# Sliding-window attention in a fused decoder block: transposed scores, no row maximum, a multiplicative decay and a row sum by matmul

## Chip, cores and metric

One Trainium2 chip, eight cores. Each core computes a quarter of one of the two sequences (2048 of 8192 positions), with no exchange between cores: the 128 positions before its own come in as an extra input. The metric is the device time of the slowest core in microseconds. Executions of a kernel agree to about 0.3% except that now and then one die, once both, runs at a lower granted clock and takes longer. Such slow runs are left out of all ratios. The medians quoted are over all runs of a kernel; the slow ones among them raise a median by at most 0.4 us, except for a_all, where only the fast runs are quoted.

## The reference, cut to what matters

```
u = rms_norm(h, norm_mix)
z = u @ w_in                       # pool input, q, k, v, two gates
y_pool = pool_mixer(u_pool, ...) @ p_pool
y_attn = swa_sink_attention(q, k, v, sinks) @ p_attn
h = h + (sigmoid(z_gp) * y_pool + sigmoid(z_ga) * y_attn) @ w_out
h = h + relu(rms_norm(h) @ w_up)**2 @ w_down
return rms_norm(h)

# swa_sink_attention: 8 query heads of 64, 2 key heads, blocks of 128 queries
# on 256 keys (previous block and own), window of 128
s = q k / 8 - slope[head] * dist         # -1e30 outside the window
m = max(max over keys of s, sink)
p = exp(s - m) / (sum exp(s - m) + exp(sink - m))
o = p @ v
```

Two identities allow the change. Subtracting m cancels between numerator and denominator, so it may be left out as long as the exps stay in range. And exp(s - slope * dist) = exp(s) * exp(-slope * dist), where the second factor depends only on head and position in the block, so it can be computed once.

## The kernel before

A core goes through stages: norm, transposes and the projections with the pooling mixer (to about 134 us in the trace), attention over 16 blocks (to 240.5), the gated mix, the output projection with the second norm, and the MLP. Only the attention stage and what it feeds on change. A helper records every operation and puts a semaphore wait wherever two engines touch the same buffer; each engine then executes its own stream in the order of the program, as the traces show (VectorE's timeline before repeats sink maximum, multiply, four additions, reduction, reciprocal, copy every 5.85 us, the order in which the loop below issues them). The parts concerned:

```python
BIAS[:, h, :]  = DM * -SLOPES[h]               # VectorE, 16 of these at the start

def att_s1(b):                                 # queries on partitions
    for h in range(8):
        mm(bank(h % 4)[...256 columns], QT[head h, block b], K or KS[256 keys])
    for j in range(4):
        tt("dve", asb[:, j:8:4, :], bank(j), bt[:, j:8:4, :], ALU.add)   # fp32
    reduce_max(mx, asb)                                                  # VectorE
def att_tiny(b):    # max with the sink, its negative, sink - max  (VectorE, POOL)
def att_exp(b):
    for h in range(8):
        act(apb[:, h, :], asb[:, h, :], AF.Exp, bias=ng[:, h], accum=rsum[:, h])
    act(es, es, AF.Exp)
def att_tr(b):      # 16 transposes of 128x128 probabilities into PSUM
def att_ptevac(b):  # 2 ScalarE copies of 128x1024 back to SBUF
def att_pv(b):      # 16 matmuls: probabilities as weights, V as 64 columns
    den = rsum + es; rd = reciprocal(den)
def att_s4_on(b):   # one VectorE multiply 128x512 from PSUM
def att_s4_t(b):    # 4 transposes of the output
def att_s4_evac(b): # VectorE copy of these into QT

for i in range(20): # blocks i .. i-3 in flight
    att_tiny(i-1); att_ptevac(i-2); att_exp(i-1); att_s4_on(i-3); att_s1(i)
    att_s4_t(i-3); att_pv(i-2); att_tr(i-1); att_s4_evac(i-3)
```

## Time and profile before

| | before |
|---|---|
| median of 15 runs | 940.48 us (the five runs at the time of the prediction: 939.69) |
| span of the profiled run, slowest core (core 2) | 937.0 us |
| attention stage on that core | 133.9 to 240.5 us |
| period of one block | 5.85 us |
| in a block: ScalarE busy, VectorE busy | 5.85 us, 5.75 us |
| granted clock in the stage | 0.55 |

How to read it: the page's slices show what is busy when, but not what ends last. A table of stretches gives each engine's busy time in one period of a stage: as long as an engine is busy for the whole period, the period cannot get shorter without less work on that engine. The groups say which instructions fill it, and the timeline's brackets (idle time before an instruction, and who ended it) say where one engine waits for another. In the views PE is TensorE's matmuls, PEld its weight loads, DVE VectorE, ACT ScalarE, POOL GpSimdE; L399 is a line of the kernel, often that of a helper that many operations share. The granted clock is the share of full speed at which TensorE ran. The prediction shows the lines for the kernel before.

### The profile page before, as it was taken

The numbers are of one execution on the slowest core, as the hardware profiler recorded it, in microseconds if no ns is written. First come the engines' busy times: TensorE is split into PE (matmuls) and PEld (weight loads), VectorE is DVE, ScalarE is ACT, GpSimd is POOL, SyncE is SP. The second block draws the span as 40 slices with busy tenths as digits, with TensorE's granted clock in tenths as the row PEclk, the third lists the DMA queues.
The fourth block names the chain that finished last, engine by engine and source line by source line (L and its number), as shares of the span: only waits on it lengthen the run. The fifth ranks groups of instructions, "written<-read, shape, count | busy, mean of one in ns | idle before, by whom it ended". The sixth has DMA issues, their size and how long they took to land.

```text
span 937.0 us, 13763 instructions; the slowest of 8 cores (934.2 to 937.0 us)
## 1 busy us (share of the span) xinstructions
PE 844.7 (90%) x4386; PEld 401.7 (43%) x4441; DVE 392.6 (42%) x582; ACT 320.9 (34%) x678; POOL 208.1 (22%) x236
## 2 busy tenths in 40 slices
PE   1589957887999999999999999999999999999994
PEld 1344423454444444444444444444444444444441
DVE  2372189999222222236542223322223232224545
ACT  2264538999322222235542211112221112223321
POOL 3021731000123232221122111211112111113333
PEclk9999985555799999999999999999999999999997
DMA  9850019300005050069608300560008300001213
GB/s 175 159 181 25 1 21 146 60 2 1 1 1 68 1 68 1 1 147 243 151 23 118 62 1 1 80 100 1 1 1 127 54 1 1 1 1 68 90 69 134
DMA packets 37397, 55.91 MB, mean 60 GB/s; under 512 B 6992, under 2 KB 21584, under 8 KB 37328
## 3 DMA queue, kind: packets, MB, share of 16 engines
q0 software_dynamic: 28816, 27.95, 21.7%
q1 hardware_dynamic: 8512, 27.09, 8.7%
q8 instruction: 37, 0.61, 0.3%
q14 instruction: 32, 0.26, 0.1%
HBM read 74.04 MB, written 8.39 MB: 88 GB/s over the span
## 4 chain that ended last, share of the span: by engine, by line
PE 73%; DVE 9%; issue 7%; ACT 6%; DMA 3%; POOL 1%; DVEq 0%; POOLq 0%; ACTq 0%
PE psum L388 70%; DVE arena L403 6%; ACT arena L399 5%; DMA arena<-w_in 3%; PE psum L392 2%; DVE arena L662 1%; ACT arena L418 1%; DVE arena L408 1%; POOL arena L403 1%; DVE arena L413 0%; POOL arena L423 0%; DVEq L194 0%; ACTq L194 0%; POOLq L280 0%; DVE arena L716 0%
## 5 line engine op out<-in xcount | busy, mean ns | idle before, releaser
L388 PE MATMUL psum<-arena 128*128 128x512 bf16 (+2 forms) x3785 | 781.8, 370 | 33.0 <-DVE arena L403 14.2
L388 PEld LDWEIGHTS psum<-arena 128*128 128x128 bf16 (+1 forms) x3840 | 361.1, 101 | 435.8 <-issue 42.7
L403 POOL TENSOR_TENSOR arena<-arena 128x512 bf16<-128x512 f32 (+3 forms) x199 | 179.8, 910 | 684.0 <-ACT arena L399 291.1
L399 ACT ACTIVATE arena<-psum 128x512 f32<-128x512 f32 (+1 forms) x208 | 123.9, 597 | 450.7 <-PE psum L388 447.7
L403 DVE TENSOR_TENSOR arena<-psum,arena 128x512 f32<-128x512 f32 (+2 forms) x241 | 177.2, 760 | 156.9 <-PE psum L388 122.1
L399 ACT ACTIVATE arena<-arena 128x256 bf16<-128x256 f32 (+2 forms) x209 | 136.8, 673 | 108.4 <-DVE arena L403 51.0
L403 DVE TENSOR_TENSOR arena<-arena 128x512 bf16<-128x512 f32 (+5 forms) x93 | 57.9, 623 | 157.0 <-ACT arena L399 152.6
L392 PE MATMUL psum<-arena 128*128 128x128 bf16 x601 | 75.6, 263 | 46.1 <-DVE arena L408 16.8
L413 DVE SCALAR_TENSOR_TENSOR arena<-arena,psum 128x512 f32<-128x512 f32 x64 | 43.9, 688 | 123.8 <-PE psum L388 120.7
L392 PEld LDWEIGHTS psum<-arena 128*128 128x128 bf16 x601 | 43.8, 111 | 85.7 <-issue 85.2
L418 ACT COPY arena<-psum 128x1024 bf16<-128x1024 bf16 (+4 forms) x57 | 43.4, 808 | 20.6 <-PE psum L388 20.6
L413 DVE SCALAR_TENSOR_TENSOR arena<-arena 128x1024 f32<-128x1024 f32 (+1 forms) x20 | 29.7, 1486 | 39.1 <-POOL arena L403 23.9
L408 DVE TENSOR_SCALAR arena<-arena 128x1 f32<-128x1 f32 (+1 forms) x82 | 24.0, 318 | 35.2 <-ACT arena L399 34.0
L662 DVE TENSOR_REDUCE arena<-arena 128x8 f32<-128x2048 f32 x16 | 36.6, 2286 | 1.7
L399 ACT ACTIVATION_READ_ACCUMULATOR arena<-arena 128x1 f32 x177 | 36.7, 208 | 0.0
L413 DVE SCALAR_TENSOR_TENSOR arena<-psum,arena 128x512 f32<-128x512 f32 x32 | 22.1, 691 | 22.6 <-PE psum L388 22.5
L423 POOL DMA_DIRECT2D arena<-w_in x14 | 12.7, 920 | 16.1 <-DVE arena L403 15.9
L399 ACT ACTIVATE arena<-psum,arena 128x512 bf16<-128x512 f32 x16 | 11.2, 781 | 5.7 <-PE psum L388 4.6
L418 ACT CAST arena<-psum 128x512 bf16<-128x512 f32 (+1 forms) x10 | 5.2, 522 | 18.3 <-PE psum L388 18.3
L423 POOL DMA_DIRECT2D arena<-w_down x4 | 3.5, 884 | 22.7 <-PE psum L388 22.7
L420 DVE COPY arena<-psum 128x512 bf16<-128x512 bf16 x16 | 6.1, 381 | 1.4 <-PE psum L392 1.4
L716 DVE RECIPROCAL arena<-arena 128x8 f32<-128x8 f32 x16 | 3.1, 194 | 2.4 <-POOL arena L403 2.4
(13 smaller groups left out, 14.4 us busy)
## 6 DMA issues: line engine op xcount, KB each, us to landing
arena<-x SPq DMA_DIRECT2D x32, 512.0 KB, 7.9
arena<-w_up POOLq DMA_DIRECT2D x4, 2048.0 KB, 18.7
arena<-w_down POOLq DMA_DIRECT2D x4, 2048.0 KB, 23.7
y<-arena SPq DMA_DIRECT2D x16, 512.0 KB, 2.6
arena<-w_in POOLq DMA_DIRECT2D x9, 512.0 KB, 11.0
arena<-w_out POOLq DMA_DIRECT2D x1, 2048.0 KB, 32.0
arena<-w_in POOLq DMA_DIRECT2D x4, 256.0 KB, 15.4
arena<-w_in POOLq DMA_DIRECT2D x1, 1024.0 KB, 30.1
```

The source lines that it names most:

```text
L388: P.op("pe", lambda e: e.matmul(out, lhsT, rhs, start=start, stop=stop), r=[lhsT, rhs], w=[out])
L392: P.op("pe", lambda e: e.transpose(out, in_, IDENT), r=[in_, IDENT], w=[out])
L399: return e.activation(out, in_, func, bias=bias, scale=scale, **kw)
L403: P.op(eng, lambda e: e.tensor_tensor(out, in0, in1, op), r=[in0, in1], w=[out])
L408: return e.tensor_scalar(out, in0, s1, None, op0)
L413: P.op(eng, lambda e: e.scalar_tensor_tensor(out, in0, scalar, in1, op0, op1), r=[in0, in1] + ([scalar] if isap(scalar) else []), w=[out])
L418: P.op("act", lambda e: e.copy(out, in_), r=[in_], w=[out])
L420: P.op(eng, lambda e: e.tensor_copy(out, in_), r=[in_], w=[out])
L423: P.op(q, lambda e: e.dma_start(out=out, in_=in_), r=[in_], w=[out], dma_slot=slot)
L662: P.op("dve", lambda e: e.reduce_max(mx, asb, AX.X), r=[asb], w=[mx])
L716: P.op("dve", lambda e: e.reciprocal(rd, den), r=[den], w=[rd])
```

## The change

The intent is to take the probability transposes out, and with them the copies, the maximum and the bias additions. Scores are computed transposed (keys on partitions, queries and heads in the free dimension), so the exps already have the orientation that the value matmul wants as weights. A query's maximum over the keys would then lie across partitions, so it is dropped; the bias becomes a factor; the row sum comes from a 65th column of ones in V.

```diff
-    BIAS/BIASZ = -slope * distance         (fp32, VectorE)
+    for h in range(8):                     (bf16, ScalarE)
+        act(EDEC[:, :, h, :], DMv, AF.Exp, scale=-SLOPES[h])
+        act(EDEC0[:, h, :], DMZ, AF.Exp, scale=-SLOPES[h])
+    act(ESINK, SINK, AF.Exp)
...
+    def att_s(b):
+        for kc in range(2):
+            for g in range(2):
+                mm(bank(kc * 2 + g), KT[rows of g, 128 keys], QT[rows of g, 4 heads x 128 queries])
+    def att_exp(b):
+        for kc in range(2):
+            act(ASB[b % 2][...], psum[two banks], AF.Exp, scale=0.125)
+    def att_decay(b):
+        for kc in range(2):
+            for g in range(2):
+                tt("dve", apt[...], asb[...], e[...], ALU.mult)         # 128x512 bf16
+    def att_pv(b):                         # V now has 65 columns, the last is 1
+    def att_norm(b):
+        for g in range(2): den = obank(g)[:, :, 64:65] + ESINK
+        rd = reciprocal(den)
+        for g in range(2): on = obank(g)[:, :, 0:64] * rd
+    def att_ot(b):                         # 4 transposes, one ScalarE copy
+
+    for i in range(19):
+        att_s(i); att_exp(i); att_decay(i-1); att_norm(i-2); att_pv(i-1); att_ot(i-2)
```

On the host side only layouts change: the query columns of w_in are reordered so that a query head sits on the partitions of its key head (which makes the swapped copy of K and its two transfers needless), and the distance tables are transposed.

More of the change, by code (lines that the diff above doesn't have):

```diff
@@ L24 @@
 BUCKET = 1024
-BIAS_TT = True
-TS_MAX = False
-FUSED_MAX = False
 def _esize(dt):
@@ L256, in _build @@
     dm_d = din("dm", [128, 256])
-    dm0_d = din("dm0", [128, 256])
+    dm0_d = din("dm0", [128, 128])
     invc_d = din("invc", [128, 64])
@@ L307, in _build @@
     KT0 = MIX0 + 32768
-    KS0 = KT0 + 4352
-    V0 = KS0 + 4352
-    WOUT0 = V0 + 4352
+    V0 = KT0 + 4352
+    WOUT0 = V0 + 8704
     C0 = WOUT0 + 16384
@@ L318, in _build @@
     KT = sb(KT0, 2176, BF16)
-    KS = sb(KS0, 2176, BF16)
-    V = sb(V0, 17 * 128, BF16).rearrange("p (t k) -> p t k", t=17)
+    V = sb(V0, 17 * 130, BF16).rearrange("p (t g k) -> p t g k", t=17, g=2)
     WOUT = sb(WOUT0, 8 * 1024, BF16).rearrange("p (c n) -> p c n", c=8)
@@ L325, in _build @@
     DM = sb(c, 256, F32); c += 1024
-    DMZ = sb(c, 256, F32); c += 1024
+    DMZ = sb(c, 128, F32); c += 512
+    ESINK = sb(c, 8, F32); c += 32
     G1 = sb(c, 8, F32); c += 32
@@ L344, in _build @@
     WS = [sb(H0 + 49152 + i * 8192, 8 * 512, BF16).rearrange("p (c n) -> p c n", c=8) for i in range(2)]
-    ASB = [sb(H0 + i * 16384, 2048, F32).rearrange("p (h k) -> p h k", h=8) for i in range(2)]
-    APN = [sb(H0 + i * 16384 + 8192, 2048, BF16).rearrange("p (h k) -> p h k", h=8) for i in range(2)]
-    APT = [sb(H0 + i * 16384 + 12288, 2048, BF16).rearrange("p (h k) -> p h k", h=8) for i in range(2)]
+    ASB = [sb(H0 + i * 12288, 2048, BF16).rearrange("p (c n) -> p c n", c=4) for i in range(2)]
+    APT = [sb(H0 + i * 12288 + 8192, 2048, BF16).rearrange("p (c h q) -> p c h q", c=4, h=4) for i in range(2)]
     TG = [[sb(H0 + s * 8192 + j * 2048, 512, F32) for j in range(4)] for s in range(2)]
@@ L371, in _build @@
     st_fix = STAT[:, 16:48]
-    def _stset(j):
-        return [STAT[:, 64 + 64 * i + 8 * j:72 + 64 * i + 8 * j] for i in range(4)]
-    st_mx, st_m8, st_ng, st_rsum, st_es, st_den, st_rd = (_stset(j) for j in range(7))
+    st_den = [STAT[:, 64 + 16 * i:72 + 16 * i] for i in range(2)]
+    st_rd = [STAT[:, 72 + 16 * i:80 + 16 * i] for i in range(2)]
     ON = [sb(H0 + 57344 + i * 1024, 512, BF16) for i in range(2)]
-    MT = sb(H0 + 59392, 1024, F32).rearrange("p (h k) -> p h k", h=8)
-    MT2 = sb(H0 + 63488, 512, F32).rearrange("p (h k) -> p h k", h=8)
     P.op("dve", lambda e: e.memset(NHALF, -0.5), w=[NHALF])
     PBS = STAT[:, 48:52]
-    NEG1 = STAT[:, 56:64]
-    P.op("dve", lambda e: e.memset(NEG1, -1.0), w=[NEG1])
     def isap(v):
@@ L432, in load_small_consts @@
         dma("sp", DMZ, dm0_d, "dm0")
+        P.op("dve", lambda e: e.memset(V[:, :, :, 64:65], 1.0), w=[V[:, :, :, 64:65]])
         dma("sp", SINK, sink_d, "sink")
@@ L474, in evac_copy @@
         cp("act", dst, src)
-    def evac_q(dst, src):
-        act(dst, src, AF.Copy, scale=0.125)
     def piece_job(wbuf, wc0, dst_fn, evac_fn, piece, after=None):
@@ L529, in v_transposes @@
                 tp(pt[:, j, :], VT[:, (t0 + j) * 128:(t0 + j + 1) * 128])
-            evac_copy(V[:, t0:t0 + nt, :], pt)
+            evac_copy(V[:, t0:t0 + nt, :, 0:64], pt.rearrange("p t (g k) -> p t g k", g=2))
     def v_chunk(p):
@@ L534, in v_chunk @@
                          after=v_transposes if p == 4 else None)
-    def v_job(t0):
-        nt = min(4, 17 - t0)
-        def fn():
-            b = next_bank()
-            o = bank(b)
-            for j in range(nt):
-                for dchunk in range(8):
-                    mm(o[:, j * 128:(j + 1) * 128], UT[:, t0 + j, dchunk, :], WS[1][:, dchunk, 128:256],
-                       start=(dchunk == 0), stop=(dchunk == 7))
-            evac_copy(V[:, t0:t0 + nt, :], o[:, 0:nt * 128].rearrange("p (t k) -> p t k", t=nt))
-        return (t0 + nt - 1, fn)
-    def ks_swap():
-        dma("sp", KS[64:128, :], KT[0:64, :], "ksa")
-        dma("sp", KS[0:64, :], KT[64:128, :], "ksb")
     def pool_chunk(g, p):
@@ L557, in k_chunk @@
     def k_chunk(p):
-        return piece_job(WS[1], 0, lambda c0, n: KT[:, c0:c0 + n], evac_copy, PIECES[p],
-                         after=ks_swap if p == 4 else None)
+        return piece_job(WS[1], 0, lambda c0, n: KT[:, c0:c0 + n], evac_copy, PIECES[p])
     def q_chunk(qc, p):
         return piece_job(WS2, qc * 128, lambda c0, n, qc=qc: QT[:, qc, c0 - 128:c0 - 128 + n],
-                         evac_q, PIECES[p])
+                         evac_copy, PIECES[p])
     jobs = []
@@ L630, in _build @@
     dma("pool", WOUT, w_out_d.rearrange("(c p) n -> p c n", p=128), "wout")
-    BIAS = sb(MIX0, 2048, F32).rearrange("p (h k) -> p h k", h=8)
-    BIASZ = sb(MIX0 + 20480, 2048, F32).rearrange("p (h k) -> p h k", h=8)
-    if FUSED_MAX or BIAS_TT:
-        for h in range(8):
-            ts("dve", BIAS[:, h, :], DM, -SLOPES[h], None, ALU.mult)
-            ts("dve", BIASZ[:, h, :], DMZ, -SLOPES[h], None, ALU.mult)
-    def att_s1(b):
-        asb = ASB[b % 2]
-        dmt = DMZ if b == 0 else DM
-        for h in range(8):
-            cc, r, g = h // 2, h % 2, h // 4
-            ksrc = KT if r == g else KS
-            o = bank(h % 4)[:, (h // 4) * 256:(h // 4) * 256 + 256]
-            mm(o, QT[r * 64:(r + 1) * 64, cc, b * 128:(b + 1) * 128],
-               ksrc[r * 64:(r + 1) * 64, b * 128:b * 128 + 256])
-        mx = st_mx[b % 4]
-        if FUSED_MAX:
-            bt = BIASZ if b == 0 else BIAS
-            for h in range(8):
-                o = bank(h % 4)[:, (h // 4) * 256:(h // 4) * 256 + 256]
-                P.op("dve", lambda e, h=h, o=o: e.tensor_tensor_reduce(
-                    out=asb[:, h, :], in0=o, in1=bt[:, h, :], scale=1.0, scalar=-3.0e38,
-                    op0=ALU.add, op1=ALU.max, accum_out=mx[:, h:h + 1]),
-                    r=[o, bt[:, h, :]], w=[asb[:, h, :], mx[:, h:h + 1]])
-        elif BIAS_TT:
-            bt = BIASZ if b == 0 else BIAS
-            for j in range(4):
-                tt("dve", asb[:, j:8:4, :], bank(j).rearrange("p (h k) -> p h k", h=2), bt[:, j:8:4, :],
-                   ALU.add)
-            P.op("dve", lambda e: e.reduce_max(mx, asb, AX.X), r=[asb], w=[mx])
-        else:
-            for h in range(8):
-                o = bank(h % 4)[:, (h // 4) * 256:(h // 4) * 256 + 256]
-                stt("dve", asb[:, h, :], dmt, -SLOPES[h], o, ALU.mult, ALU.add)
-            if TS_MAX:
-                for h in range(8):
-                    P.op("dve", lambda e, h=h: e.tensor_scalar(asb[:, h, :], asb[:, h, :], 1.0, None,
-                                                              ALU.mult, ALU.max, accum_out=mx[:, h:h + 1]),
-                         r=[asb[:, h, :]], w=[asb[:, h, :], mx[:, h:h + 1]])
-            else:
-                P.op("dve", lambda e: e.reduce_max(mx, asb, AX.X), r=[asb], w=[mx])
@@ L675, in att_tiny @@
-    def att_tiny(b):
-        k4 = b % 4
-        mx, m8, ng, es = st_mx[k4], st_m8[k4], st_ng[k4], st_es[k4]
-        tt("dve", m8, mx, SINK, ALU.max)
-        tt("pool", ng, m8, NEG1, ALU.mult)
-        tt("pool", es, SINK, m8, ALU.subtract)
-    def att_exp(b):
-        k4 = b % 4
-        asb, apb = ASB[b % 2], APN[b % 2]
-        ng, rsum, es = st_ng[k4], st_rsum[k4], st_es[k4]
-        for h in range(8):
-            act(apb[:, h, :], asb[:, h, :], AF.Exp, bias=ng[:, h:h + 1], accum=rsum[:, h:h + 1])
-        act(es, es, AF.Exp)
@@ L690, in att_tr @@
-    def att_tr(b):
-        apb = APN[b % 2]
-        for half in range(2):
-            pt = bank_bf(4 + half).rearrange("p (h k) -> p h k", h=4)
+    EDEC = sb(MIX0, 2048, BF16).rearrange("p (c h q) -> p c h q", c=2, h=8)
+    EDEC0 = sb(MIX0 + 20480, 1024, BF16).rearrange("p (h q) -> p h q", h=8)
+    DMv = DM.rearrange("p (c q) -> p c q", c=2)
+    for h in range(8):
+        act(EDEC[:, :, h, :], DMv, AF.Exp, scale=-SLOPES[h])
+        act(EDEC0[:, h, :], DMZ, AF.Exp, scale=-SLOPES[h])
+    act(ESINK, SINK, AF.Exp)
@@ new lines, in att_s @@
+    def att_s(b):
+        for kc in range(2):
+            for g in range(2):
+                rows = slice(g * 64, (g + 1) * 64)
+                mm(bank(kc * 2 + g), KT[rows, (b + kc) * 128:(b + kc + 1) * 128],
+                   QT[rows, :, b * 128:(b + 1) * 128])
+    def att_exp(b):
+        for kc in range(2):
+            act(ASB[b % 2][:, 2 * kc:2 * kc + 2, :],
+                psum[:, kc * 1024:(kc + 1) * 1024].rearrange("p (c n) -> p c n", c=2), AF.Exp, scale=0.125)
+    def att_decay(b):
+        asb, apt = ASB[b % 2], APT[b % 2]
+        for kc in range(2):
+            e = EDEC0 if (b == 0 and kc == 0) else EDEC[:, kc, :, :]
+            for g in range(2):
+                tt("dve", apt[:, 2 * kc + g, :, :],
+                   asb[:, 2 * kc + g, :].rearrange("p (h q) -> p h q", h=4), e[:, g * 4:g * 4 + 4, :], ALU.mult)
@@ L694, in att_tr, with obank @@
+    def obank(g):
+        return bank(4 + g)[:, 0:260].rearrange("p (h k) -> p h k", h=4)
+    def att_pv(b):
+        apt = APT[b % 2]
+        for g in range(2):
             for hh in range(4):
-                h = half * 4 + hh
                 for kc in range(2):
-                    tp(pt[:, hh, kc * 128:(kc + 1) * 128], apb[:, h, kc * 128:(kc + 1) * 128])
-    def att_ptevac(b):
-        apt = APT[b % 2]
-        for half in range(2):
-            pt = bank_bf(4 + half).rearrange("p (h k) -> p h k", h=4)
-            cp("dve" if (FUSED_MAX and half == 1) else "act", apt[:, half * 4:half * 4 + 4, :], pt)
@@ L705, in att_pv @@
-    def att_pv(b):
-        k4 = b % 4
-        apt = APT[b % 2]
-        rsum, es, den, rd = st_rsum[k4], st_es[k4], st_den[k4], st_rd[k4]
-        ob = bank(6)
-        for h in range(8):
-            g = h // 4
-            for kc in range(2):
-                mm(ob[:, h * 64:(h + 1) * 64], apt[:, h, kc * 128:(kc + 1) * 128],
-                   V[:, b + kc, g * 64:(g + 1) * 64], start=(kc == 0), stop=(kc == 1))
-        tt("pool", den, rsum, es, ALU.add)
-        P.op("dve", lambda e: e.reciprocal(rd, den), r=[den], w=[rd])
@@ L718, in att_s4_on @@
-    def att_s4_on(b):
-        on, rd = ON[b % 2], st_rd[b % 4]
-        ob = bank(6)
-        tt("dve", on.rearrange("p (h d) -> p h d", h=8), ob.rearrange("p (h d) -> p h d", h=8),
-           rd.unsqueeze(2).to_broadcast([128, 8, 64]), ALU.mult)
-    def att_s4_t(b):
-        on = ON[b % 2]
-        pt7 = bank_bf(7)[:, 0:512].rearrange("p (c k) -> p c k", c=4)
-        for cc in range(4):
-            tp(pt7[:, cc, :], on[:, cc * 128:(cc + 1) * 128])
-    def att_s4_evac(b):
-        pt7 = bank_bf(7)[:, 0:512].rearrange("p (c k) -> p c k", c=4)
-        cp("dve", QT[:, :, b * 128:(b + 1) * 128], pt7)
@@ L734, in blk @@
-    def blk(j):
-        return 0 <= j < 16
-    for i in range(20):
-        if blk(i - 1):
-            att_tiny(i - 1)
-        if blk(i - 2):
-            att_ptevac(i - 2)
-        if blk(i - 1):
-            att_exp(i - 1)
-        if blk(i - 3):
-            att_s4_on(i - 3)
-        if blk(i):
-            att_s1(i)
-        if blk(i - 3):
-            att_s4_t(i - 3)
-        if blk(i - 2):
-            att_pv(i - 2)
-        if blk(i - 1):
-            att_tr(i - 1)
-        if blk(i - 3):
-            att_s4_evac(i - 3)
+                    mm(obank(g)[:, hh, :], apt[:, 2 * kc + g, hh, :], V[:, b + kc, g, :],
+                       start=(kc == 0), stop=(kc == 1))
@@ new lines, in att_norm @@
+    def att_norm(b):
+        den, rd, on = st_den[b % 2], st_rd[b % 2], ON[b % 2]
+        for g in range(2):
+            tt("dve", den[:, g * 4:g * 4 + 4].unsqueeze(2), obank(g)[:, :, 64:65],
+               ESINK[:, g * 4:g * 4 + 4].unsqueeze(2), ALU.add)
+        P.op("dve", lambda e: e.reciprocal(rd, den), r=[den], w=[rd])
+        for g in range(2):
+            tt("dve", on[:, g * 256:(g + 1) * 256].rearrange("p (h d) -> p h d", h=4), obank(g)[:, :, 0:64],
+               rd[:, g * 4:g * 4 + 4].unsqueeze(2).to_broadcast([128, 4, 64]), ALU.mult)
@@ new lines, in att_ot @@
+    def att_ot(b):
+        pt = bank_bf(6 + b % 2)[:, 0:512].rearrange("p (c k) -> p c k", c=4)
+        for cc in range(4):
+            tp(pt[:, cc, :], ON[b % 2][:, cc * 128:(cc + 1) * 128])
+        cp("act", QT[:, :, b * 128:(b + 1) * 128], pt)
+    for i in range(19):
+        if i < 16:
+            att_s(i)
+            att_exp(i)
+        if 0 <= i - 1 < 16:
+            att_decay(i - 1)
+        if 0 <= i - 2 < 16:
+            att_norm(i - 2)
+        if 0 <= i - 1 < 16:
+            att_pv(i - 1)
+        if 0 <= i - 2 < 16:
+            att_ot(i - 2)
@@ L756, in _build @@
+    phase_end('D')
     OT = QT
-    phase_end('D')
     for pr in range(4):
@@ L886, in _consts @@
 def _consts():
-    qi = np.arange(128)[:, None]
-    kj = np.arange(256)[None, :]
-    dist = (128 + qi - kj).astype(np.float32)
-    valid = (dist >= 0) & (dist < 128)
-    dm = np.where(valid, dist, np.float32(1e32)).astype(np.float32)
-    dm0 = dm.copy()
-    dm0[:, :128] = np.float32(1e32)
+    kk = np.arange(128)[:, None]
+    qi = np.arange(128)[None, :]
+    far = np.float32(1e32)
+    prev = np.where(kk > qi, qi - kk + 128, far).astype(np.float32)
+    own = np.where(kk <= qi, qi - kk, far).astype(np.float32)
+    dm = np.concatenate([prev, own], axis=1)
+    dm0 = np.full((128, 128), far, np.float32)
     ident = np.eye(128, dtype=np.float32)
@@ L900, in _consts @@
         inv_first[:, g, :] = (np.float32(1.0) / cnt)[None, :]
-    return dm, dm0, ident, inv_mid.reshape(128, 64), inv_first.reshape(128, 64)
+    return dm, dm0, prev, ident, inv_mid.reshape(128, 64), inv_first.reshape(128, 64)
 def kernel(x, norm_mix, w_in, pool_w, pool_b, pool_scale, attn_sinks, p_pool, p_attn,
@@ L920, in make_in_maps @@
     x = f(x)
-    dm, dm0, ident, inv_mid, inv_first = _consts()
+    dm, dm0, prev, ident, inv_mid, inv_first = _consts()
+    w1 = f(w_in[0]).copy()
+    wq = w1[:, 512:1024].reshape(D, 2, 4, 64)
+    w1[:, 512:1024] = wq.transpose(0, 2, 1, 3).reshape(D, 512)
     shared = {
-        "w_in": f(w_in[0]), "pool_w": f(pool_w[0]), "p_pool": f(p_pool[0]), "p_attn": f(p_attn[0]),
+        "w_in": w1, "pool_w": f(pool_w[0]), "p_pool": f(p_pool[0]), "p_attn": f(p_attn[0]),
         "w_out": f(w_out[0]), "w_up": f(w_up[0]), "w_down": f(w_down[0]),
@@ L943, in make_in_maps @@
             m["xh"] = f(x[b, ch * T - 128:ch * T])
-            m["dm0"] = dm
+            m["dm0"] = prev
             m["invc"] = inv_mid
```

## The prediction

> **What bounds the kernel now.** I read the page's busy table by slices first, then a table of stretches, then the instruction groups and the timeline of one attention block, then the chain of waits. On the page:
>
> ```profile
> PE   1589957887999999999999999999999999999994
> DVE  2372189999222222236542223322223232224545
> ACT  2264538999322222235542211112221112223321
> PEclk9999985555799999999999999999999999999997
> ```
>
> Each digit is a fortieth of the span (23.4 us), in tenths. Over most of the span PE is at 9 and everything else is low: that part is matmul streaming at full clock, and the change does not touch it. Slices 6 to 9 are the exception: DVE and ACT at 9, PE at 7 to 8, the granted clock at half. That is the attention stage, the only one the diff rewrites. The table of stretches (length; busy us of PE, PEld, DVE, ACT, POOL; clock; DMA share; GB/s), cut at two successive DVE reductions so that each of the first two rows is one block, and then at the end of the stage:
>
> ```profile
> 211.60:217.45 5.85, 4.89 (x45) 3.06 (x44) 5.75 (x9) 5.85 (x21) 0.52 (x3) 0.50 0.01 1
> 217.45:223.30 5.85, 4.84 (x45) 2.99 (x44) 5.75 (x9) 5.85 (x21) 0.52 (x3) 0.50 0.00 0
> 234.00:240.50 6.50, 4.49 (x43) 2.89 (x41) 2.01 (x4) 4.38 (x14) 0.20 (x1) 0.50 0.02 4
> 240.50:244.00 3.50, 3.50 (x11) 1.30 (x10) 0.42 (x1) 0.00 (x0) 0.00 (x0) 0.51 0.00 0
> ```
>
> A block takes 5.85 us; ACT is busy for all of it, DVE for 5.75. So two engines bound the stage together, and relieving only one would bring nothing. The next stage's first matmul starts at 240.5 us and runs at half clock until about 244. Which instructions fill a block, from the groups of two blocks (busy us, mean ns):
>
> ```profile
> L399 ACT ACTIVATE arena<-arena 128x256 bf16<-128x256 f32 x17 | 8.5, 539 | 0.0
> L403 DVE TENSOR_TENSOR arena<-psum,arena 128x512 f32<-128x512 f32 x8 | 4.9, 677 | 0.0
> L662 DVE TENSOR_REDUCE arena<-arena 128x8 f32<-128x2048 f32 x2 | 4.6, 2286 | 0.2
> L418 ACT COPY arena<-psum 128x1024 bf16<-128x1024 bf16 x4 | 3.9, 1042 | 0.0
> ```
>
> ACT per block: eight exps, 0.49 us apart in the timeline (3.9 us), and two probability copies out of PSUM, together 1.9 us. DVE per block: four bias additions (2.48 us), the maximum (2.29 us), and a normalising multiply, a copy and three small ones. How the stage begins:
>
> ```profile
> 134.70 2.79 ACT L399 ACTIVATE arena<-psum,arena 128x512 bf16<-128x512 f32 x4 [4.59 <-PE psum L388]
> 144.77 0.51 ACT L399 ACTIVATE arena<-arena 128x256 bf16<-128x256 f32 x1 [7.29 <-POOL arena L403]
> ```
>
> ACT finishes the pooling outputs at 137.5 and has its first exp at 144.77. In that gap DVE builds the bias (16 scalings), adds it and takes the maximum. The chain of waits inside the stage goes through DVE and ACT alternately (reduction 31.3%, additions 30.0%, the ACT copy 14.4%), not through PE.
>
> [...] PSUM activations of 512 and copies of 1024 elements differ by 1024 - 597 = 427 ns, 0.834 per element; with bias and scale pointers the 512 form takes 781. [...] eight 64-row matmuls of 256 columns finish in 1.04 to 1.08 us, less than 0.14 each[...]. [...]
>
> **The change, part by part.** Scores are now computed transposed (keys on partitions), so the exps give the probabilities already in the orientation the value matmul needs. No maximum is subtracted; the bias becomes a product with a precomputed decay; the row sum comes from a ones column in V.
>
> ACT per block. Removed: eight exps with their accumulator reads and one for the sink (4.0 us), two 1024 copies (1.9). Added: two 1024-element exps straight from PSUM, sized like the copies (1.02 each, 1.9 as a pair), and the output transposes' copy, 128x512 bf16 (0.61). New sum 2.5 us.
>
> DVE per block. Removed: four additions, the maximum, the small sink maximum, the copy. Added: four products 128x512 all in bf16 SBUF[...]; successive DVE instructions overlap by 0.08 (2.48 us for four of 0.68)[...]. The normalisation: two tiny additions (0.16 as the 128x8 form, about 0.25 together), reciprocal 0.19, two 256-element multiplies from PSUM[...] (0.76 together), plus two hand-overs to itself of 0.17 as seen before the sink maximum: 1.54. New sum 3.0 us.
>
> PE per block. Removed: 16 probability transposes. The scores become four 512-column matmuls in row-group pairs (2 x 0.43 = 0.85 cold); values are 16 matmuls as before (1.06), now 65 columns; the four output transposes stay (0.5). New sum 2.4 us.
>
> No engine alone asks for more than 3.0 us. But the order of the code makes a loop: the scores of block i+1 stand behind the value matmuls of i-1 and the output transposes of i-2 in PE's stream, and both wait for norm(i-2). Followed from the end of norm(i-2), with 0.15 per hop between engines (DVE end to PE start in the timeline): value matmuls (they start when the first half is normalised) done at 0.9; transposes until 1.35; first score pair done at 1.8; exp of both halves 2.0 to 3.95; last two products until 4.85; norm(i) until 6.35. That is two blocks: 3.15 to 3.2 us per block, just above DVE's 3.0. I take 3.15.
>
> The start. ACT now builds the decay after 137.5: eight pairs of 256 and 128 elements. [...] 0.33 + 0.23 each pair, 4.5 us, and the sink's 0.1. First exp at 142.1, 2.7 us earlier than now. Blocks 0 and 1 have no normalisation, which gains about 1.6 us.
>
> The end. Last exp at 142.1 + 15 x 3.15 - 1.6 = 187.8; from there exps, products, norm(14), values, norm(15), transposes: 1.95 + 0.9 + 1.55 + 0.9 + 1.7 + 0.5 = 7.5. The next stage starts at 195.3 instead of 240.5: 45.2 us gained, all on the path, because that stage's matmuls are next in PE's stream. Its weights are no obstacle: the DMA table shows the loads landed by about 172. From there to the end the code is the same, 697 us at full clock. If PE is warm at that point, the half-clock start (3.4 us, worth 1.7) shrinks; I count 0.5. Sum: 939.7 - 45.2 - 0.5 = 894.0.
>
> **The rivals.** [...] Then they cost 2.48 like the additions and DVE needs 4.0 us per block: 15 x 0.85 = 13 us later, about 907. For it: nothing here shows the fast form. [...] *The loop through PE binds harder than I count,* because score banks are single and each hop costs more: 3.6 per block, about 901. For it: six hops in the loop. *The clock recovers,*[...]: the PE part of the loop falls by some 0.4 us per block and DVE's 3.0 binds, about 891; with smaller DVE gaps 2.75 per block, 888. *It is hidden anyway,* because the stage waits for weights or the next stage is limited elsewhere: against it stand the DMA table and PE at 9 right after 240.5. That would give about 935; I give it very little.
>
> **Range and chances.** [...] the warm clock with small gaps the lower: 887 to 906. Even twice my period's excess leaves over 2% (920.9), so faster 0.97.
>
> **What would show it right or wrong.** Right: four bf16 products near 0.42 us, ACT no longer full, DVE the busiest of the stage near 95%, blocks 3.0 to 3.3 us apart, the gated stage starting near 195 and the rest shifted unchanged. Wrong: products at 0.69; PE waiting for ACT before each score; DVE idle by more than 0.5 us per block; a first exp later than 143; or a later stage that grew longer.

Some passages of the prediction are cut where the marks stand, because no trace of the kernel before and no run of this case shows what they said. The sum is what it came to, 939.7 - 45.2 - 0.5 = 894.0 us, but terms of it are missing. In VectorE's 3.0 us per block the time of one bf16 product is cut, and with it the step to 1.45 us for four. It was the assumption leaned on most, and no trace showed such an instruction at that time; the changed kernel's trace gives 0.419 us. The time of one multiply of 256 elements, behind the 0.76 that stands, is cut too; the trace before gives an estimate of 0.42 us, on a straight line between 0.158 us for the sink maximum of 8 elements and 0.68 for an addition of 512. The way to the 0.33 + 0.23 us per pair of decay activations is cut; the same comes out of the 220 ns of the 8-element exp, the 0.834 ns per element that stands above and the 0.09 us by which successive activations overlap in ScalarE's timeline (144.77 + 0.51 against a next start at 145.19). The 0.5 us for the half-clock start of the next stage (a clock of 0.50 from 240.5 to 243.9 us) was a guess. The first rival is that the products take as long as the additions (0.677 us each); it just about sets the upper end of the range.

## The result

The changed kernel takes 892.08 us (median of 9 runs, 891.09 to 892.66 without the slow one), against 940.48 before. The ratio is 0.9488 with a 95% interval of 0.9478 to 0.9497. Here and below a ratio is the mean time of one kernel's fast runs over that of the other's from the same rounds, so it is not quite the ratio of the medians quoted. The result is correct.

The page of the changed kernel, busy tenths in fortieths of its span (here 22.3 us each) and the granted clock:

```profile
PE   1389975679999999999999999999999999999994
DVE  2273265852223222466322332223322233224545
ACT  2263547842222222355421111211112211123322
PEclk9999995769999999999999999999999999999997
```

Of the four slices at half clock three are left, at 0.5 to 0.7, and in them neither VectorE nor ScalarE is at 9 any more. The rest looks the same. To compare like with like I read core 2 in both traces (the page above is of core 3, the slowest of its run, whose first stage ended 1 us later). On core 2 the pooling outputs' operands are ready at 133.9 us in both. The table of stretches of core 2 (length; busy us of PE, PEld, DVE, ACT, POOL with counts; clock; DMA share; GB/s): two successive blocks, the end of the stage, and the start of the next:

```profile
152.62:155.26 2.64, 1.58 (x24) 1.28 (x24) 2.43 (x10) 1.86 (x2) 0.00 (x0) 0.50 1.36 154
155.26:158.76 3.50, 3.29 (x29) 1.55 (x28) 2.63 (x11) 3.19 (x5) 0.00 (x0) 0.50 1.19 133
186.24:192.95 6.71, 3.54 (x47) 2.79 (x46) 4.86 (x17) 3.11 (x4) 0.00 (x0) 0.50 0.00 0
192.95:198.00 5.05, 5.05 (x15) 1.81 (x14) 0.00 (x0) 1.18 (x2) 0.00 (x0) 0.54 0.01 3
```

Early in the stage blocks come in pairs of 2.64 and 3.50 us, 6.14 for two, where before one took 5.85; from about 168 us on every block of this core takes 3.0 to 3.1 us, with almost the same sum. The next stage's first matmul starts at 192.95 instead of 240.5, 47.6 us earlier; the span of this core went from 937.0 to 889.6, 47.4 us. So the whole gain was made in the attention stage and was kept to the end. The groups of these two blocks (busy us, mean ns):

```profile
L388 ACT ACTIVATE arena<-psum 128x1024 bf16<-128x1024 f32 x5 | 4.9, 1021 | 0.2
L392 DVE TENSOR_TENSOR arena<-arena 128x512 bf16<-128x512 bf16 x9 | 3.4, 419 | 0.7 <-ACT arena L388 0.7
...
L392 DVE TENSOR_TENSOR arena<-psum,arena 128x256 bf16<-128x256 f32 x4 | 1.5, 418 | 0.2
...
L407 ACT COPY arena<-psum 128x512 bf16<-128x512 bf16 x2 | 1.2, 586 | 0.9 <-PE psum L381 0.9
```

Every new instruction has the duration that was estimated for it: the exp 1.02 us, the bf16 product 0.42, the half multiply 0.42, the copy 0.59. (A block has two exps; the fifth started in the next one.) The start of the stage in ScalarE's timeline of core 2:

```profile
137.58 4.24 ACT L388 ACTIVATE arena<-arena 128x256 bf16<-128x256 f32 x17
141.72 3.91 ACT L388 ACTIVATE arena<-psum 128x1024 bf16<-128x1024 f32 x4
```

The 17 activations that build the decay run from 137.58 on, and the first scores' exp starts at 141.72, where before the first exp was at 144.77. Last, why blocks alternate, in VectorE's timeline of core 2 (start, length, instruction, and in brackets the idle time before it and who ended it):

```profile
157.16 0.76 DVE L392 TENSOR_TENSOR arena<-arena 128x512 bf16<-128x512 bf16 x2 [0.51 <-ACT arena L388]
158.08 0.76 DVE L392 TENSOR_TENSOR arena<-arena 128x512 bf16<-128x512 bf16 x2 [0.15 <-ACT arena L388]
...
160.06 1.42 DVE L392 TENSOR_TENSOR arena<-arena 128x512 bf16<-128x512 bf16 x4
```

In this first part, in every second block the products wait for both exps (0.51 and 0.15 us); in the others all four run through in 1.42 us. That is the shape of a loop over two blocks. Later the waiting is shared out: in each block the second pair of products waits 0.15 us, the first pair under 0.15.

Core 2 is not the rule for all cores. From the first exp to the next stage's first gate matmul it needs 51.2 us, the longest of the eight, with the lowest clock (0.54 from 145 to 185 us); core 5 needs 49.5 us, the shortest, with the highest clock (0.73). That too is what a loop through TensorE would do.

### The profile page after: what moved, and what is told of

The parts are those of the page before. It is cut to its first block, busy times and chain, and to the rows that moved or that the text cites. A ratio compares the mean times of both kernels' runs of the same rounds, so it can differ in the third digit from the quotient of the medians.

```text
span 891.0 us, 12377 instructions; the slowest of 8 cores (886.5 to 891.0 us)
## 1 busy us (share of the span) xinstructions
PE 804.6 (90%) x4121; PEld 374.8 (42%) x4121; DVE 335.1 (38%) x566; ACT 271.1 (30%) x439; POOL 199.2 (22%) x188
## 4 chain that ended last, share of the span: by engine, by line
PE 78%; DVE 7%; issue 5%; ACT 4%; DMA 3%; POOL 1%; POOLq 0%; DVEq 0%; ACTq 0%; SPq 0%
PE psum L377 75%; DVE arena L392 5%; ACT arena L388 4%; DMA arena<-w_in 3%; PE psum L381 2%; DVE arena L397 1%; POOL arena L392 1%; DMA arena<-x 1%; DVE arena L402 1%; POOL arena L412 0%; DVE arena L645 0%; DVEq L191 0%; POOLq L277 0%; ACT arena L407 0%; ACTq L191 0%
## 5 line engine op out<-in xcount | busy, mean ns | idle before, releaser
L377 PEld LDWEIGHTS psum<-arena 128*128 128x128 bf16 x3776 | 353.7, 100 | 461.8 <-issue 70.2
L388 ACT ACTIVATE arena<-psum 128x512 f32<-128x512 f32 (+1 forms) x224 | 145.4, 658 | 437.5 <-PE psum L377 433.9
L392 DVE TENSOR_TENSOR arena<-psum,arena 128x512 f32<-128x512 f32 (+2 forms) x225 | 143.4, 653 | 155.6 <-PE psum L377 119.9
L392 DVE TENSOR_TENSOR arena<-arena 128x512 bf16<-128x512 bf16 (+5 forms) x141 | 79.3, 584 | 169.5 <-ACT arena L388 166.1
L388 ACT ACTIVATE arena<-arena 128x1024 bf16<-128x1024 f32 (+1 forms) x82 | 74.4, 929 | 101.4 <-DVE arena L392 50.7
L381 PE MATMUL psum<-arena 128*128 128x128 bf16 x345 | 32.0, 240 | 26.9 <-DVE arena L422 10.5
L381 PEld LDWEIGHTS psum<-arena 128*128 128x128 bf16 x345 | 23.7, 107 | 40.8 <-issue 40.4
L397 DVE TENSOR_SCALAR arena<-arena 128x1 f32<-128x1 f32 x66 | 19.0, 304 | 37.3 <-ACT arena L388 36.4
L407 ACT COPY arena<-psum 128x512 bf16<-128x512 bf16 (+3 forms) x41 | 22.0, 553 | 31.5 <-PE psum L377 21.8
L407 ACT CAST arena<-psum 128x512 bf16<-128x512 f32 (+1 forms) x26 | 14.6, 561 | 31.0 <-PE psum L377 31.0
L388 ACT ACTIVATE arena<-psum,arena 128x512 bf16<-128x512 f32 x16 | 11.2, 781 | 5.9 <-PE psum L377 5.9
L388 ACT ACTIVATION_READ_ACCUMULATOR arena<-arena 128x1 f32 x49 | 9.1, 186 | 0.0
```

The source lines that it names most:

```text
L377: P.op("pe", lambda e: e.matmul(out, lhsT, rhs, start=start, stop=stop), r=[lhsT, rhs], w=[out])
L381: P.op("pe", lambda e: e.transpose(out, in_, IDENT), r=[in_, IDENT], w=[out])
L388: return e.activation(out, in_, func, bias=bias, scale=scale, **kw)
L392: P.op(eng, lambda e: e.tensor_tensor(out, in0, in1, op), r=[in0, in1], w=[out])
L397: return e.tensor_scalar(out, in0, s1, None, op0)
L407: P.op("act", lambda e: e.copy(out, in_), r=[in_], w=[out])
```

## The experiments

Twelve kernels ran, each timed against the kernel before on the same chip. The changed kernel was not run again in these lots, so a gain over its 892.08 us is a difference between lots: the fast medians of the kernel before differ by 0.7 us between the lots, and the 95% interval of a variant's ratio to before reaches 1.4 to 2.6 us to each side. The first three take parts of the work out of the kernel before; the rest alter the changed kernel. In short:

| run | median us | ratio to before | result |
|---|---|---|---|
| changed kernel | 892.08 | 0.9488 | correct |
| b_nomax | 938.05 | 0.9984 | correct |
| b_nocopy | 937.94 | 0.9981 | wrong |
| b_both | 907.92 | 0.9655 | wrong |
| a_f32decay | 903.28 | 0.9609 | correct |
| a_deep | 888.34 | 0.9442 | correct |
| a_merged | 890.76 | 0.9482 | correct |
| a_early | 888.06 | 0.9450 | correct |
| a_hoist | 887.28 | 0.9440 | correct |
| a_warm | 887.81 | 0.9442 | correct |
| a_warmT | 888.24 | 0.9438 | correct |
| a_all | 878.2 (two fast runs of four) | 0.9340 | correct |
| a_all2 | 876.71 | 0.9323 | correct |

### Do two engines bound the stage before?

The theory: VectorE and ScalarE bind together, so relieving one brings nothing. The rivals: one of them alone binds.

b_nomax, the kernel before without its largest VectorE instruction:

```diff
-            P.op("dve", lambda e: e.reduce_max(mx, asb, AX.X), r=[asb], w=[mx])
-        tt("dve", m8, mx, SINK, ALU.max)
-        tt("pool", ng, m8, NEG1, ALU.mult)
-        tt("pool", es, SINK, m8, ALU.subtract)
+        tt("pool", ng, ZERO8, NEG1, ALU.mult)
+        tt("pool", es, SINK, ZERO8, ALU.subtract)
```

> The kernel before, without the maximum: VectorE loses 2.29 us (the reduction) and 0.15 us per block, ScalarE keeps its 5.85. Theory (two engines bound the stage together): ScalarE still takes 5.85 us per block, so the period stays; only the first exp comes about 2.4 us earlier. Time 936 to 939 us. Rival (VectorE alone binds, since the reduction is 31% of the chain of waits in the stage): the period falls towards 4 us and the time to about 912. The result stays correct.

Two blocks of its stage, in the table of stretches:

```profile
200.00:211.70 11.70, 10.26 (x90) 5.83 (x88) 6.96 (x14) 11.70 (x39) 1.05 (x7) 0.50 0.01 2
```

VectorE fell from 5.75 to 3.48 us per block, ScalarE is still busy for all of the 11.70 us, and the period did not move. Time 938.05, 0.16% less, within the noise (the interval reaches 1.0001). The reduction made up 31.3% of the chain of waits in the stage, and taking it out brought nothing: a chain passes through one of two equally long engines and doesn't show the other.

b_nocopy, the kernel before without the two ScalarE copies (the value matmul reads pooling data that lies in SBUF anyway, so the result is wrong):

```diff
-            att_ptevac(i - 2)
-        apt = APT[b % 2]
+        apt = PMT[:, b % 2, :].rearrange("p (h k) -> p h k", h=8)
```

> The kernel before, without the two ScalarE copies of the probabilities out of PSUM (the value matmul reads other data already there, so the result is wrong on purpose): ScalarE falls from 5.85 to about 4.0 us per block, VectorE keeps 5.75. Theory (both bind): the period goes from 5.85 to about 5.75, the time to 936 to 939 us. Rival (ScalarE alone binds): the period falls towards 4 us and the time to about 911.

```profile
200.00:211.70 11.70, 9.10 (x88) 5.91 (x86) 11.32 (x19) 8.02 (x35) 1.03 (x6) 0.59 0.01 2
```

The mirror image: ScalarE now has 8.02 of 11.70 us and waits, VectorE 11.32, period unchanged, time 937.94.

b_both takes both out, with the two edits above.

> The kernel before, without the maximum and without the copies (wrong result on purpose). Theory (both bind): only now the period falls, to ScalarE's 4.0 or to TensorE's matmuls and transposes at half clock, 4.0 to 4.7 us per block, and the time to 908 to 920 us. If each of the two alone had already brought that, the theory is wrong; if this one too stays near 937, something else binds.

```profile
160.00:180.00 20.00, 15.67 (x220) 10.39 (x219) 17.33 (x36) 20.00 (x86) 2.57 (x15) 1.00 0.67 105
```

Now ScalarE is full again at a period of 4.03 us (its accumulating exps alone) and the time is 907.92, a hair below the expected range. The theory stands: none for one, none for the other, 32 us for both. This is why a change that touched only the maximum or only the transposes would have looked worthless. One thing in that line was not expected and is taken up below: the clock is 1.00 (0.90 to 0.97 over the eight cores from 145 to 200 us), with all 20 transposes per block still there.

### Are the products faster because all is bf16, and does it matter?

a_f32decay holds the factors in fp32, so one operand of three has 4 bytes:

```diff
-    EDEC = sb(MIX0, 2048, BF16)...
+    EDEC = sb(MIX0, 2048, F32)...          # EDEC0 likewise
```

> The changed kernel with the decay factors held in fp32 instead of bf16, so that the 64 products have one 4-byte operand. Theory ([...] VectorE or the loop through it binds): each product goes from 0.42 to 0.69 us, VectorE needs 2.64 + 4 x 0.27 = 3.7 us per block, more than the present 3.0 mean, and the time rises by about 11 us from 892 to about 903. Rival (VectorE has slack that hides it, the loop through TensorE binds): the loop holds two of four products per two blocks, 0.27 us per block, time about 896. If the products stay at 0.42, the data type is not what matters.

```profile
L392 DVE TENSOR_TENSOR arena<-arena 128x512 bf16<-128x512 bf16 x62 | 38.5, 682 | 0.0
```

(The group's name gives the bf16 operand only.) One 4-byte operand takes the products from 0.42 to 0.68 us, idle time before them falls to zero, and the stage from first exp to the next stage's first gate matmul takes 61.9 us on each of the eight cores. So VectorE alone binds, and the time is 903.28: 11.2 us more, as the theory gave. The rival of the prediction in which the products take as long as the additions before (0.677 us) is thereby built and measured; it had been put at 907.

### Is there a loop through TensorE?

a_deep issues scores and exps one block further ahead:

```diff
-    ASB = [... for i in range(2)]
+    ASB = [sb(H0 + o, ...) for o in (0, 4096, 12288)]     # and b % 3 in place of b % 2
-    for i in range(19):
-        att_s(i); att_exp(i)
+    att_s(0); att_exp(0)
+    for i in range(19):
+        att_s(i + 1); att_exp(i + 1)
```

> The changed kernel with the scores and exps one block further ahead (a third score buffer in SBUF), so that the scores no longer stand behind the normalisation of the same round in TensorE's stream. Theory (the two-block loop through TensorE, 6.13 us at half clock, makes the period 3.07 where VectorE alone needs 2.64): the period falls to 2.64 to 2.70 whatever the clock, the next stage starts 5 us earlier, time 886 to 888 us. Rival (VectorE's waits on ScalarE and its own hand-overs bind, not the loop): time stays within 890 to 893.

VectorE's timeline in three successive blocks:

```profile
155.29 1.42 DVE L392 TENSOR_TENSOR arena<-arena 128x512 bf16<-128x512 bf16 x4
...
157.94 1.42 DVE L392 TENSOR_TENSOR arena<-arena 128x512 bf16<-128x512 bf16 x4
...
160.58 1.42 DVE L392 TENSOR_TENSOR arena<-arena 128x512 bf16<-128x512 bf16 x4
```

The waits for the exps are gone and the period is 2.64 us, VectorE's own sum, in every block. The period moved as the theory said and the time fell by 3.7 us to 888.34, slightly less than the 4 to 6 expected. Nothing about any instruction was altered, only the order and the third score buffer that it needs, so the order set the period of the changed kernel.

The clock rose as well (to 0.75 to 0.80 over the cores), which could be a rival cause. The trace speaks against it: from 171 to 177 us core 2 is at 0.50, and its blocks still take 2.64 us. And from the first exp to the next stage's first gate matmul all eight cores need 46.7 to 46.8 us, whatever their clock, where the changed kernel needs 49.5 to 51.2 us, 50.4 on average.

a_merged keeps the order and uses two products of 1024 instead of four of 512:

```diff
-            for g in range(2):
-                tt("dve", apt[:, 2 * kc + g, ...], asb[:, 2 * kc + g, ...], e[:, g * 4:g * 4 + 4, :], ALU.mult)
+            tt("dve", apt[:, 2 * kc:2 * kc + 2, ...], asb[:, 2 * kc:2 * kc + 2, :], e, ALU.mult)
```

> The changed kernel with two products of 1024 elements instead of four of 512 per block. Theory: [...] two take 1.30 against 1.42; per two blocks 0.12 (the block in which VectorE runs through) and 0.07 (the block in which the second half waits for its exp) are gained, 1.5 us in all, time about 890.5 us. If VectorE were not in the loop at all, no gain.

```profile
L392 DVE TENSOR_TENSOR arena<-arena 128x1024 bf16<-128x1024 bf16 x32 | 21.9, 691 | 13.5 <-ACT arena L388 13.2
```

Each takes 0.691 us (two that run through take 1.28 in a_all), and the median fell by 1.3 us, close to the 1.5 expected. But this gain in time is not shown: by the ratios to the kernel before it is 0.6 us, the two intervals (0.9467 to 0.9497 and 0.9478 to 0.9497) overlap almost wholly, and the runs scatter from 889.95 to 892.78. In the profiled run of each the stage is 1.0 us shorter on the average of the eight cores (49.4 instead of 50.4 us).

### The start and the end of the stage

a_early moves the building of the decay, unchanged but for its address, in front of the last projection jobs:

```diff
+    (the 17 activations, EDEC at MIX0 + 8192)
     while ji < len(jobs):
         jobs[ji][1]()
...
-    (the 17 activations)
```

> The changed kernel with the decay factors built on ScalarE before the last projection jobs, where ScalarE has idle time, instead of between the pooling outputs and the first exp. Theory (the 4.24 us of decay building are on the path): the first exp starts at about 137.6 instead of 141.7 and the time falls by about 4 us to 888. Rival (something else holds the stage's start, the scores or the loads that run at that time, or the projections are delayed): less than 2 us gained.

ScalarE's timeline (on core 1):

```profile
134.63 2.79 ACT L388 ACTIVATE arena<-psum,arena 128x512 bf16<-128x512 f32 x4 [4.83 <-PE psum L377]
137.30 3.98 ACT L388 ACTIVATE arena<-psum 128x1024 bf16<-128x1024 f32 x4
```

The exps follow the pooling outputs at once, and the time falls by 4.0 us for 4.24 us of decay building: within the noise all of it was on the path.

a_hoist issues the next stage's first gate matmuls around the last value matmuls:

```diff
+        if i == 16: gates(0)               # 8 matmuls of 512 into bank 0
         att_pv(i - 1)
+        if i == 16: gates(1)               # 8 more into bank 1
```

> The changed kernel with the next stage's first 16 gate matmuls issued around the last value matmuls, into score banks that are free by then. Theory (TensorE idles about 3 us through the last two normalisations and then runs the next stage's first 12 to 13 matmuls at half clock, 5.1 us in the trace): they fill that idle time and warm the clock, time 886 to 889 us. Rival (they delay the last value matmuls and so the end of the stage): less than 2 us gained.

TensorE's timeline at the end of the stage (on core 5):

```profile
188.43 0.62 PE L381 MATMUL psum<-arena 128*128 128x128 bf16 x4
188.84 4.58 PE L377 MATMUL psum<-arena 128*128 128x512 bf16 x32
193.26 0.61 PE L381 MATMUL psum<-arena 128*128 128x128 bf16 x8
193.71 6.64 PE L377 MATMUL psum<-arena 128*128 128x512 bf16 x30
```

The 32 matmuls from 188.84 are the 16 gate matmuls and, between them, the last block's 16 value matmuls; after the last transposes the next stage goes on without its half-clock start (30 matmuls in 6.64 us, 0.22 each). Gain 4.8 us; how much of it is the filled idle time and how much the clock, no run separates.

### What the clock is worth, and what raises it

a_warm adds two matmuls of 512 columns per block that nobody reads, where TensorE would wait; a_warmT adds eight transposes with as many columns instead:

```diff
+        for _ in range(2):                                        # a_warm
+            mm(bank(7), UT[:, 1, 0, :], UT[:, 1:5, 0, :])
+        for j in range(8):                                        # a_warmT
+            tp(bank_bf(7)[:, j * 128:(j + 1) * 128], UT[:, 1, j, :])
```

> The changed kernel with two idle-time matmuls of 512 columns per block whose result nobody reads, in the gap where TensorE waits for the normalisation (one output-transpose bank instead of two makes room). Theory ([...] at full clock the loop through TensorE falls below VectorE's 2.64): clock near 1 through the stage and at the next stage's start, period 2.64 to 2.75, time 885 to 888 us. Rival (more TensorE work only lengthens the loop): 892 or more.

```profile
150.00:170.00 20.00, 15.15 (x196) 7.58 (x194) 18.27 (x66) 17.57 (x23) 0.00 (x0) 1.00 1.15 151
```

> The same with eight 128x128 transposes of as many columns in place of the two matmuls. If transposes do not count as activity for the clock,[...] the clock stays near the present 0.55 to 0.65 and the time at 891 to 894 us; if they count, clock and time come out as in the run with matmuls, 885 to 888 us. The earlier run without maximum and copies, at a clock of 1.00 with 20 transposes per block, speaks for the latter.

```profile
150.00:170.00 20.00, 15.44 (x237) 10.31 (x236) 18.02 (x67) 17.75 (x23) 0.00 (x0) 1.00 1.15 155
```

These lines are of the slowest core of each run. From 145 to 185 us all eight cores of both runs have a clock of 0.94 to 1.00, where the changed kernel has 0.54 to 0.73, and the times are 887.81 and 888.24. More work for TensorE made the kernel 4 us faster. The traces show where: from the first exp to the next stage's first gate matmul 47.3 and 47.9 us pass on average instead of 50.4, and the mean clock over the next stage's first 5 us is 0.92 in both instead of 0.63 (on two cores of a_warm and three of a_warmT it is still below 0.8). And transposes do it as well as matmuls: the lowest clock of a core is 0.94 in both runs. Why the clock was near half in the changed kernel's stage is not shown; in a_warm too TensorE waits 0.6 to 0.8 us in a block, at a clock of 1.00.

### All together

a_all joins a_deep, a_merged, a_early and a_hoist; a_all2 also joins the two additions and the two multiplies of the normalisation across both output banks:

```diff
-        for g in range(2): tt("dve", den[g], obank(g)[:, :, 64:65], ESINK[g], ALU.add)
+        tt("dve", den, both banks [:, :, :, 64:65], ESINK, ALU.add)      # multiply likewise
```

> The changed kernel with all four of the earlier edits: scores one block further ahead, products of 1024 elements, decay built early, gate matmuls hoisted. Each alone gained 3.7, 1.3, 4.0 and 4.8 us against 892.1. Theory (they remove different pieces of the same path: the period, VectorE's own work, the start, the end): nearly additive, 877 to 880 us. Rival (the period becomes bound by ScalarE's 2.5 us and the deeper order and the hoist share their gain at the end): 881 to 884 us.

> As the run with all four, and the normalisation done in one addition and one multiply over both output banks instead of two each. VectorE per block falls by another 0.2 us, to about 2.3; ScalarE's 2.5 us should then be the bound, so a gain of 0 to 1.5 us on the run with all four: 876 to 880 us. If the value matmuls, which then cannot start after the first half, bind instead, it is slower.

a_all had two slow runs of four (its median of 901.39 mixes them in); its fast runs took 878.17 and 878.19, a gain of 13.9 us against 13.8 for the sum of the four single gains (13.9 against 13.0 by the ratios). a_all2 takes 876.71, and in its stage the bound has come back to ScalarE:

```profile
150.00:170.00 20.00, 13.56 (x199) 7.79 (x196) 18.13 (x43) 20.00 (x27) 0.00 (x0) 1.00 1.15 153
```

ScalarE 20.00 of 20.00, VectorE 18.13, a block every 2.38 us. It has the lowest time, though its interval (0.9301 to 0.9346) overlaps that of a_all (0.9313 to 0.9367), so its own step is not clear of noise. Its ratio of 0.9323 to the kernel before over the changed kernel's 0.9488 makes 0.983, 1.7% less than the changed kernel.

## Why the prediction was right

Predicted 894.0 with a range of 887 to 906; measured 892.08. Point by point:

- **What bounds the stage**: two engines together, shown by b_nomax, b_nocopy and b_both.
- **Durations of the added instructions**: all within 0.03 us. The bf16 product was the assumption leaned on most, one that no trace showed then; it is 0.419 against 0.42 assumed, and a_f32decay shows what it was worth.
- **VectorE's sum of 3.0 us per block** was too high: 2.64 in a_deep, where it runs alone. The products were right (1.45 predicted, 1.42 measured). The normalisation was put at 1.54 and takes 1.39, since its two hand-overs cost 0.10 to 0.11 and not 0.17 each; and the 0.08 overlap between successive instructions, counted inside the two groups, was forgotten between them (twice 0.08).
- **The loop over two blocks** was put at 6.3 us (6.35 followed through) and measured 6.14 at half clock; a_deep shows that it was the bound on all cores. That 0.16 over seven and a half pairs is about 1.2 us.
- **Start**: first exp at 142.1 predicted, 141.72 measured; a_early shows that it lies on the path. Gain of the first two blocks: 1.6 predicted; from the first exp (141.72) to the third (146.14) 4.42 us passed instead of 6.14, so 1.7.
- **End**: 7.5 us from the last exp to the next stage predicted, 6.71 measured (186.24 to 192.95).
- **The clock**: this step failed. The prediction credited 0.5 us for a warmer start of the next stage. On core 2 it was colder: 5.05 us at 0.54 where the kernel before has 3.50 at 0.51, at half speed a loss of about 0.8 us more. Over all cores it was no warmer either: the mean clock of the next stage's first 5 us went from 0.68 to 0.63. The three small overestimates above (0.4, 1.2 and 0.8 us) outweigh this miss of 1.3 us. So the mechanism was right, but part of the closeness of the number is luck: errors of both signs cancelled.
- **"VectorE the busiest near 95%"** failed too: it is busy 38.5 of 45.8 us on core 2, 84%, because the loop makes its products wait for the exps. The prediction's own numbers were 3.0 in a loop of 3.15; with VectorE's sum at 2.64 the slack is wider.
- **The rivals**: the products did not take as long as the additions (0.419 against 0.677 us); the loop binds, but not harder than counted; the clock recovered only in part (0.54 on this core, 0.54 to 0.72 over the cores between 142.5 and 190 us); that fewer transposes would be the reason, the runs do not show: eight added ones raised the clock as added matmuls did, to 0.94 to 1.00 (a_warmT, a_warm). Where it did recover, the period followed: on core 3 the clock is 1.00 from 168.5 to 176.6 us, and the three blocks there take 2.64, 2.82 and 2.64 us. Nothing was hidden, as the equal gains at the stage's end and at the span's end show.
- **Slips in its reading**, without effect on the sum: it counts the slices from 0, and in the first of its four ScalarE is at 8, not 9; the "additions 30.0%" are the share of a helper's line that the normalising multiply and the sink maximum go through too; and the 16 scalings of the bias begin at 134.0 us, 3.5 us before the gap in which it places them.

## What to carry to other kernels

When two engines are each busy for a whole period, a chain of waits that names one of them is no guide: sum both per period, and expect nothing from a change that relieves only one. After such a change look for the loop that program order makes between engines: here a different order, with one more buffer, brought the period from 3.07 to VectorE's own 2.64 us. And ask what the first and the last iteration put on the path, since the start and the end of the stage were together worth about twice the loop (8.8 against 3.7 us).

## What the runs show of the clock and of VectorE

- Transposes and the clock: eight added transposes per block raised the stage's clock from 0.54 to 0.73 over the cores to 0.94 to 1.00, just as matmuls of the same number of columns did (a_warmT, a_warm), and b_both ran at 0.90 to 0.97 with 20 transposes per block.
- Waits, columns and the clock: in the changed kernel's stage on core 2 the longest wait of TensorE for another engine was 1.4 us, and the clock was 0.54; in a_warm TensorE waited 0.6 to 0.8 us in each block of 2.7 us, and the clock was 1.00. What went with the clock was the density of streamed columns, transposes included and the pairs of 64-row score matmuls counted once (four of 512 columns take 1.04 us together in the changed kernel, where the 128-row ones of 512 columns follow each other by 0.43 us, both at a clock of 0.50). In columns per period, and clock over the middle of the stage on the eight cores: a_f32decay 2576 per 3.71 us, 694 per us, 0.50; before 4608 per 5.85, 788, 0.56 to 0.62; changed 2576 per 3.07, 839, 0.54 to 0.73; a_deep 2576 per 2.64, 976, 0.75 to 0.80; b_both 4608 per 4.03, 1143, 0.90 to 0.97. This is an order in five kernels whose ranges partly overlap, not a tested rule; what sets the clock stays open.
- VectorE's products: all in bf16 one of 512 elements takes 0.419 us (the changed kernel) and one of 1024 takes 0.691 (a_merged); with one fp32 operand one of 512 takes 0.682 (a_f32decay).
- A VectorE instruction that needs the result of the one before it: 0.10 to 0.17 us of idle time here (0.10 to 0.11 between a_deep's additions, reciprocal and multiplies; 0.17 before the first sink maximum of the kernel before), against an overlap of 0.08 without such a need.
